# A two-block network on one core: the queue from which keys, queries and values are loaded back from DRAM

## The chip, the cores and the metric

The kernel runs on one core of a Trainium2 chip. The core has a matrix engine (TensorE, PE in the rows), a vector engine (VectorE, DVE), a scalar engine (ScalarE, ACT), a general engine (GpSimd, POOL) and SyncE (SP), which computes nothing and here only starts transfers. Each engine works off its own list of instructions in order; an instruction may wait for a semaphore that another engine or a transfer raises. A transfer between DRAM and the core's memory (SBUF) is started by an instruction on some engine's list and then runs beside it. The metric is the device time of the core, in microseconds (us); lower is better.

## The reference

The input is 512 tokens of width 1024, and for the second block 256 context tokens. Everything is fp32. In short:

```python
def first_block(x, c, ...):
    for l in range(2):                       # two hybrid layers
        h = rms_norm(x, gain) * (1 + scale) + shift        # scale, shift, gate from silu(c) @ w_mod
        aq, ak, av, ag, rq, rk, rv, rg, gq, gk, gv, gg, ga = split(h @ w_in)
        a = sliding_window_attention(rotary(aq), rotary(ak), av, sinks) * silu(ag)  # 8 heads, 2 of keys
        r = rms_norm(retention(rotary(rq), rotary(rk), rv)) * silu(rg)              # 4 heads
        g = rms_norm(gated_linear_attention(gq, gk, gv, log_a)) * silu(gg)          # GLA, 4 heads
        x = x + gate * rms_norm(concat([a, r, g]) @ w_out)

def second_block(x, c, ctx, ...):
    # layer 0, "even": windowed attention over tokens and context, and latent attention (8 heads),
    #   for the 512 tokens and for the 256 context tokens; then an FFN for each
    # layer 1, "odd": grouped attention (8 heads) and differential attention (4 heads)
    #   over context and tokens; then an FFN
    for l in range(2):
        h, hc = modulated rms_norm of x, xc
        y, yc = (mixer_even, mixer_odd)[l](h, hc, ...)
        x = x + g1 * rms_norm(y)
        x = x + g2 * rms_norm(swiglu(modulated rms_norm(x)))
        # layer 0 only: the same two steps for the context xc with yc
```

## The kernel before

The program is written in Python against a framework whose scheduler decides the order of each engine's list, from the order in which the code issues the operations and from its own estimate of when each will be ready. Pools of tiles with a fixed number of buffers set when a tile may be written again.

*Products.* Each fp32 operand is split into a high part that TensorE takes at its faster precision and a low part, the rest; a product is three matmuls (line 389: high x high, low x high, high x low). Weights come in units of 128 x up to 1024 elements. `weights` (lines 413 to 426) handles one: a transfer from DRAM into `wr` (line 417, three buffers), the high part `wh` by a cast on ACT (line 422, two buffers), the low part `wl` by a subtraction on POOL (line 398) or DVE (line 400). Some 370 such units pass in the whole program, so ACT has a cast of weights every few microseconds.

*Attention.* The projections give their results with features on the partitions, four heads to a tile. The rotation (`rope`) makes rotated pieces, each split in high and low. `put` (line 803) stores the pieces to a scratch tensor in DRAM, in an order that sorts them by head: `rq0`, `rk0`, `rv0`, `aq0`, `ak0`, `av0` for layer 0 of the first block, `rq1` and so on for layer 1, `eqm`, `eka`, `ekn`, `ekp`, `evb`, `eqc`, `eqpc` and others for the even layer, `oqc`, `okc`, `okd` and others for the odd one. `get` (line 806) loads the keys, queries and values of one head back into SBUF, where the products of attention and retention read them. Between a store and its get lies the wait for the store's landing in DRAM. The names on the left of a row are the tiles that a get fills: `rq`, `rk`, `rv` in retention (`retention`, line 1155), `wk`, `wq`, `wv` in the sliding windows, `ek`, `eq`, `ev` in the even layer's windows and latent attention, `ck`, `cq`, `cv` in the same for the context, `gk`, `gq`, `dk` in the odd layer.

*Stages.* In the first block, a layer projects (`layer1`), then runs GLA, whose chain of small steps is woven together with projections of the remaining units, with retention and with the sliding window. In a GLA step, ACT computes the exponentials of the decay factors (line 1068, tile `f`) and casts small operands (line 1087, tile `qb`). In the second block, projection, windows, latent attention, output projection and FFN follow each other; the context attention lies at about 900 to 980 us.

*Transfers.* Every transfer in the program stands on SP's list: the weight units, 128 transfers of modulation weights (line 738, tile `mr`) that come in the background, the stores, the gets, tables for the rotation (lines 1016 and 1024), and retention's decay masks (line 1165, into a buffer of tag `rq`). There are 1169 of them. The program counts their completions in eight counters, `DMAHW0` to `DMAHW7` in the rows of order, which it takes in turn: a transfer whose counter is still held by an earlier one waits for that one first.

```python
def put(self, dst, src):                                     # 802
    self.nc.sync.dma_start(dst, ...)                         # 803
def weights(self, src, n, where=None):                       # 413
    raw = self.tl(self.sb, [128, 1024], F32, "wr", 3)        # 415
    nc.sync.dma_start(raw[:, :n], src)                       # 417
    nc.scalar.copy(hi[:, :n], raw[:, :n])                    # 422
```

Of the kernel before, what the change touches and what calls it, by code (L numbers as in the profile page):

```python
# [11 lines left out]
F32 = mybir.dt.float32  # L12
# [187 lines left out]
class Net:  # L200
# [602 lines left out]
        self.nc.sync.dma_start(dst, src if src.dtype == F32 else src.bitcast(F32))  # L803

    def get(self, dst, src):
        self.nc.sync.dma_start(dst.bitcast(F32), src)

    def q_put(self, scr, pieces, h0, n=4, r=32):

# [1146 lines left out]
```

## Time and profile before

| what | value |
|---|---|
| device time, median of 3 runs | 2879.4 us (2874.68 to 2889.54) |
| the profiled execution: device time | 2882.13 us |
| its span, first to last instruction | 2880.3 us |
| mean granted clock of TensorE | 0.91 of full speed |
| busy, share of the span: PE, DVE, ACT, POOL | 86%, 44%, 41%, 37% |
| moved from and to DRAM | 398 MB, mean 139 GB/s |

Busy means that an instruction of that engine was being executed; starting a transfer, waiting and branching do not count. An engine's share is a mean over the whole span and hides stretches in which it is much busier. Of a transfer, the trace gives the time that its queue took to issue it and when its packets moved. The idle time ahead of an instruction is put down to what ended last before it: an instruction of another engine, a transfer, or "issue", when nothing that the profile shows was waited for.

### The profile page before, as it was taken

The page shows a single profiled execution, that of the slowest core. Times are in us where ns is not written, and L with a number is a line of the kernel's source. Part 1 is how long each engine was busy: PE and PEld are TensorE (multiplying, and loading weights), DVE is VectorE, ACT ScalarE, POOL GpSimd, SP SyncE. Part 2 cuts the span into 40 slices and gives each one's busy share as a digit, 9 for nine tenths or more (in the row PEclk, how much of TensorE's full clock was granted, in tenths as well). Part 3 has the DMA queues.
Part 4 walks back from the last instruction along what each step waited for, and adds up shares of the span by engine and source line. Part 5 has one row for each costly group of instructions (what it writes and reads, how often), then busy time and mean ns, then how long its engine had stood idle before and what let it go on. Part 6 is the DMA issues. An engine that isn't in the chain of part 4 may idle for free. (4 is left out here: it accounts for less than half of the span.)

```text
span 2880.3 us, 35460 instructions
## 1 busy us (share of the span) xinstructions
PE 2473.7 (86%) x13052; PEld 2008.7 (70%) x13052; DVE 1267.5 (44%) x2065; ACT 1187.0 (41%) x2227; POOL 1077.7 (37%) x754
## 2 busy tenths in 40 slices
PE   6887888677979987669999899999878969799997
PEld 4765566566657765548998777777766757588886
DVE  3645356335646644356453631222635647421212
ACT  2533355333537534346554422222434536333222
POOL 2434325334623551123455632323541221433334
PEclk9988889788989987779999999999888979899999
DMA  7454544435344553335653544453442254333332
GB/s 239 131 189 143 182 132 160 139 111 169 108 128 138 188 188 119 117 107 139 178 161 136 172 145 162 146 183 115 160 135 96 86 159 114 113 110 97 101 95 74
DMA packets 170817, 400.58 MB, mean 139 GB/s; under 512 B 19378, under 2 KB 60820, under 8 KB 167316
## 3 DMA queue, kind: packets, MB, share of 16 engines
q1 hardware_dynamic: 170644, 398.31, 42.6%
q8 instruction: 104, 1.70, 0.2%
q14 instruction: 69, 0.57, 0.1%
HBM read 339.85 MB, written 58.39 MB: 138 GB/s over the span
## 5 line engine op out<-in xcount | busy, mean ns | idle before, releaser
L398 POOL TENSOR_TENSOR wl<-wr,wh 128x1024 fp32r<-128x1024 f32 (+3 forms) x245 | 537.0, 2193 | 890.8 <-ACT wh L422 435.5
L422 ACT CAST wh<-wr 128x1024 fp32r<-128x1024 f32 (+3 forms) x367 | 353.4, 963 | 745.8 <-PE d L389 290.1
L389 PE MATMUL d<-hh,wh 128*128 128x512 f32 x960 | 405.6, 422 | 20.3 <-ACT hh L556 7.8
L389 PE MATMUL d<-hl,wh 128*128 128x512 f32 x960 | 399.1, 416 | 3.3 <-POOL hl L398 1.4
L389 PE MATMUL d<-hh,wl 128*128 128x512 f32 x960 | 261.8, 402 | 0.0
L400 DVE SCALAR_TENSOR_TENSOR wl<-wr,wh 128x1024 fp32r<-128x1024 f32 (+3 forms) x122 | 151.5, 1242 | 226.5 <-PE d L389 96.3
L389 PEld LDWEIGHTS d<-hh,wh 128*128 128x128 f32 x960 | 192.4, 200 | 72.1 <-issue 12.1
L389 PEld LDWEIGHTS d<-hl,wh 128*128 128x128 f32 x960 | 192.0, 200 | 45.9 <-issue 4.9
L389 PEld LDWEIGHTS d<-hh,wl 128*128 128x128 f32 x960 | 184.7, 194 | 40.6 <-issue 2.5
L921 POOL TENSOR_TENSOR oy<-pg,pg 64x256 f32<-64x256 f32 (+1 forms) x72 | 57.4, 797 | 299.9 <-DVE pg L919 95.6
L400 DVE SCALAR_TENSOR_TENSOR pg<-b,pg 128x512 fp32r<-128x512 f32 (+1 forms) x208 | 137.3, 666 | 67.7 <-ACT pg L404 66.1
L389 PE MATMUL b<-hh,wh 128*128 128x512 f32 x416 | 165.2, 397 | 0.0
L389 PE MATMUL b<-hl,wh 128*128 128x512 f32 x416 | 164.0, 394 | 0.0
L404 ACT CAST pg<-b 128x512 fp32r<-128x512 f32 (+1 forms) x208 | 117.3, 571 | 88.9 <-PE b L896 83.4
L869 DVE TENSOR_REDUCE sm<-s 128x1 f32<-128x768 f32 (+3 forms) x144 | 121.1, 847 | 65.0 <-PE s L389 64.2
L389 PE MATMUL d<-hc,wh 128*128 128x256 f32 x656 | 104.4, 309 | 24.9 <-DVE rp L400 12.5
L937 DVE SCALAR_TENSOR_TENSOR rp<-rp,d 128x512 f32<-128x512 f32 (+1 forms) x77 | 46.8, 607 | 165.0 <-ACT rp L936 164.9
L389 PE MATMUL d<-hid,wh 128*128 128x512 f32 (+1 forms) x528 | 117.6, 365 | 1.9 <-POOL hid L398 1.5
L1725 DVE SCALAR_TENSOR_TENSOR rp<-rp,b 128x512 f32<-128x512 f32 (+1 forms) x64 | 38.1, 595 | 175.8 <-PE b L389 175.3
L389 PEld LDWEIGHTS d<-hc,wh 128*128 128x128 f32 x656 | 94.0, 209 | 30.2 <-ACT wh L422 12.1
L389 PE MATMUL b<-hid,wh 128*128 128x512 f32 (+1 forms) x528 | 110.4, 360 | 0.0
L389 PEld LDWEIGHTS d<-hid,wh 128*128 128x128 f32 x528 | 90.1, 191 | 21.2 <-issue 2.9
(412 smaller groups left out, 5191.3 us busy)
## 6 DMA issues: line engine op xcount, KB each, us to landing
wr<-in_ffn_w_in SPq DMA_DIRECT2D x132, 512.0 KB
mr<-in_ada_w SPq DMA_DIRECT2D x96, 512.0 KB
wr<-in_ffn_w_out SPq DMA_DIRECT2D x48, 512.0 KB
x<-x SPq DMA_DIRECT2D x20, 1024.0 KB
wr<-in_w_in SPq DMA_DIRECT2D x38, 512.0 KB
mr<-in_w_mod SPq DMA_DIRECT2D x32, 512.0 KB
wr<-in_ev_w_in SPq DMA_DIRECT2D x20, 512.0 KB
wr<-in_ffn_w_out SPq DMA_DIRECT2D x24, 384.0 KB
```

The source lines that it names most:

```text
L389: self.nc.tensor.matmul(out, lhsT, rhs, start=start, stop=stop)
L398: self.nc.gpsimd.tensor_sub(out, src, hi)
L400: self.nc.vector.scalar_tensor_tensor(out, src, scale, hi, op0=ALU.mult, op1=ALU.subtract)
L404: self.nc.scalar.copy(hi, src)
L422: nc.scalar.copy(hi[:, :n], raw[:, :n])
L869: nc.vector.reduce_max(c, s, axis=AX.X, negate=True)
L921: nc.gpsimd.tensor_tensor(d, sel(t), sel(rs), op=ALU.mult)
L937: nc.vector.scalar_tensor_tensor(t, t, 1.0, ps, op0=ALU.add, op1=ALU.mult)
L1725: nc.vector.scalar_tensor_tensor(g, g, 0.5, pu, op0=ALU.mult, op1=ALU.mult)
```

## The change

```diff
--- before.py
+++ after.py
@@ -803,7 +803,7 @@
         self.nc.sync.dma_start(dst, src if src.dtype == F32 else src.bitcast(F32))
 
     def get(self, dst, src):
-        self.nc.sync.dma_start(dst.bitcast(F32), src)
+        self.nc.scalar.dma_start(dst.bitcast(F32), src)
 
     def q_put(self, scr, pieces, h0, n=4, r=32):
```

All 322 gets now stand on ACT's list; SP keeps 847 transfers, the stores among them. No instruction is added or removed. The scheduler orders every engine's list anew: 1125 rows of ACT's order differ, and 2306 of PE's. The pieces below give, for each instruction, its line, its operation, the tile it writes and the one it reads with the numbers that the program gives them, its size, and in brackets the semaphores that it waits for: `DMAHW` a transfer, `PE`, `DVE`, `Pool`, `Activation` an engine.

*Place 1: layer 1 of the first block, in GLA.* Before, SP's list reads as follows from the stores of retention's rotated queries to those of the keys:

```order
L803 DMA rq1_4256<-rp_1095_4928 4x32x512 [waits DVE_49]
L803 DMA rq1_4256<-rp_1101_4963 4x32x512 [waits DVE_49]
L417 DMA wr_1140_5169<-in_w_tok_b 128x768 [waits DMAHW5_49,DMAHW4_49]
L417 DMA wr_1143_5199<-in_w_tok_b 128x768 [waits DMAHW6_49,Pool_49]
L806 DMA rq_1180_5382<-rq1_4256 128x512 [waits DMAHW2_49,DMAHW3_49,DMAHW1_49,DMAHW0_49]
L1165 DMA rq_1183_5390<-in_decay 128x512 [waits DMAHW7_49]
L417 DMA wr_1166_5309<-in_w_in 128x1024 [waits Pool_49]
L803 DMA rk1_4257<-rp_1118_5052 4x32x512 [waits Activation_49]
L803 DMA rk1_4257<-rp_1110_5011 4x32x512 [waits DVE_49]
```

The first get here, row five, waits for the four counters of the stores above it; behind it stand the decay mask, a weight unit and the stores of the keys. The same get, of `rq_1180`, stands on ACT's list after the change, here between two casts of weight units:

```order
L404 CAST rp_1103_4969<-rp_1095_4928 128x512 [waits Pool_49]
L404 CAST rp_1104_4972<-rp_1101_4963 128x512 [waits DMAHW4_49,Pool_49]
L422 CAST wh_1135_5111<-wr_1134_5109 128x768 [waits DMAHW6_49,PE_49]
L806 DMA rq_1180_5382<-rq1_4256 128x512 [waits DMAHW2_49,DMAHW3_49,DMAHW1_49,DMAHW0_49]
L422 CAST wh_1138_5141<-wr_1137_5139 128x768 [waits DMAHW7_49,DVE_49,PE_49]
L1068 ACT_TABLE_LOAD
L1068 ACTIVATE f_1120_5062<-b_1121_5063 128x384 [waits PE_49]
```

It has moved behind the cast of `wh_1135` and ahead of that of `wh_1138` and of the exponentials of `f_1120`. A little further down ACT's list after the change, the four gets of the keys stand around two weight casts:

```order
L404 CAST pg_1175_5358<-pg_1173_5354 128x256 [waits Pool_49]
L806 DMA rk_1181_5384<-rk1_4257 64x512 [waits DMAHW7_49,DMAHW3_49,DMAHW1_49]
L422 CAST wh_1141_5171<-wr_1140_5169 128x768 [waits DMAHW4_49,PE_49,Activation_49]
L806 DMA rk_1181_5384<-rk1_4257 64x512 [waits DMAHW0_49]
L806 DMA rk_1182_5387<-rk1_4257 64x512 [waits DMAHW4_49,DMAHW2_49]
L806 DMA rk_1182_5387<-rk1_4257 64x512
L422 CAST wh_1144_5201<-wr_1143_5199 128x768 [waits DMAHW5_49,PE_49,Activation_49]
```

Three of the four gets lie between the casts of `wh_1141` and `wh_1144`; on SP they stood together, behind the tables of line 1016.

*Place 2: layer 0 of the first block, in GLA.* The difference of ACT's order, with the numbers of buffers left out, first at the queries of head 0 of retention:

```order
 L422 CAST wh_1082<-wr_1080 128x768
 L404 CAST pg_1238<-pg_1234 128x256
-L1087 CAST qb_130_775<-pg_1054 32x2x128 x4
+L1087 CAST qb_130_775<-pg_1054 32x2x128
+L806 DMA rq_1354<-rq_544 128x512
+L1087 CAST qb_130_775<-pg_1054 32x2x128 x3
 L404 CAST pg_1332<-pg_1328 128x256
```

The get has come between the first and the second of four small casts of GLA. Twenty rows further, at the keys of the same head:

```order
 L404 CAST rp_1028<-rp_1019 128x512
 L422 CAST wh_1142<-wr_1140 128x768
-L1087 CAST qb_128_773<-pg_1236 32x2x128 x4
+L806 DMA rk_1356<-rk_545 64x512 x2
+L806 DMA rk_1359<-rk_545 64x512 x2
+L1087 CAST qb_128_773<-pg_1236 32x2x128 x3
 L422 CAST wh_1172<-wr_1170 128x768
+L1087 CAST qb_128_773<-pg_1236 32x2x128
```

The four key gets have come ahead of the next four casts of this kind. For the next head, ACT's order after the change, from the cast that feeds a store of the attention's keys (`ak0`) to the decay factors:

```order
L404 CAST rp_232_1312<-rp_233_1313 128x512 [waits DMAHW5_49,Pool_49]
L806 DMA rk_323_1671<-rk0_545 64x512 [waits DMAHW6_49,PE_49]
L806 DMA rq_322_1669<-rq0_544 128x512 [waits DMAHW0_49,PE_49]
L404 CAST pg_283_1491<-pg_282_1489 128x128 [waits DVE_49,Activation_49]
L806 DMA rk_323_1671<-rk0_545 64x512 [waits DMAHW2_49]
L806 DMA rk_324_1674<-rk0_545 64x512 [waits DMAHW4_49]
L806 DMA rk_324_1674<-rk0_545 64x512 [waits DMAHW6_49]
L806 DMA rv_326_1679<-rv0_548 128x4x128 [waits DMAHW7_49,PE_49]
L1068 ACTIVATE f_286_1499<-b_287_1500 128x384
L1068 ACTIVATE f_286_1499<-b_288_1504 128x384
```

Queries, keys and values of the head are now loaded from here, and the last get, of `rv_326`, waits for counter `DMAHW7` ahead of the exponentials of `f_286`. On SP's list after the change the stores that these wait for stand here:

```order
L738 DMA mr_285_1498<-in_w_mod 128x1024 [waits DMAHW3_49,DMAHW0_49,PE_49]
L738 DMA mr_300_1558<-in_w_mod 128x1024 [waits DMAHW5_49,DMAHW4_49,PE_49]
L803 DMA ak0_547<-rp_232_1312 2x32x512 [waits Activation_49]
L803 DMA ak0_547<-rp_232_1312 2x32x512 [waits DMAHW7_49]
L803 DMA ak0_547<-rp_233_1313 2x32x512 [waits DMAHW1_49,DVE_49]
```

The second store of `ak0` is the one that takes counter `DMAHW7`; it stands behind two transfers of modulation weights.

*Place 3: the context attention of the second block.* A piece of the difference of ACT's order, at the context's queries, keys and values:

```order
+L806 DMA ck_7460<-eka 64x256 x2
+L806 DMA ck_7463<-eka 64x256 x2
 L623 COPY y_6703<-d_7383 128x512
+L806 DMA cq_7466<-eqc 128x256
+L806 DMA cq_7468<-eqc 128x256
+L806 DMA cq_7470<-eqc 128x256
+L806 DMA cq_7472<-eqc 128x256
+L806 DMA cv_7474<-eva 128x2x128
+L806 DMA ck_7563<-eka 64x256
 L503 ACTIVATE rp_7458<-oy_6699 128x512
+L806 DMA ck_7563<-eka 64x256
+L806 DMA ck_7566<-eka 64x256 x2
```

Gets come in ahead of the exponential of line 503 and of the softmax that follows it, eleven in this piece; 86 lie in this stretch in all.

## Rows read from the trace of the kernel before

**Rows 1.** Page, part 1: busy time, share of the span and count of each engine.
```profile
PE 2473.7 (86%) x13052; PEld 2008.7 (70%) x13052; DVE 1267.5 (44%) x2065; ACT 1187.0 (41%) x2227; POOL 1077.7 (37%) x754
```

**Rows 2.** Two windows: length, busy time and count per engine, then clock, DMA share, GB/s.
```profile
560.00:810.00 250.00, 198.86 (x935) 156.61 (x934) 123.23 (x208) 100.91 (x205) 108.08 (x96) 0.88 0.40 131
900.00:980.00 80.00, 70.72 (x393) 55.99 (x393) 45.61 (x99) 50.61 (x141) 33.25 (x32) 0.94 0.57 180
```

**Rows 3.** Line 806: ns to issue (minimum/median/maximum), first and last start; who waited for it.
```profile
L806 SPq DMA_DIRECT2D ck<-ekn x32: 444/567/597, 915.9 to 965.7; - x32
...
L806 SPq DMA_DIRECT2D cq<-eqpc x16: 444/590/1681, 918.9 to 957.8; - x16
...
L806 SPq DMA_DIRECT2D cv<-evb x8: 376/380/587, 920.1 to 970.7; - x8
...
L806 SPq DMA_DIRECT2D eq<-eqm x8: 319/432/4920, 1079.3 to 1167.2; - x8
...
  PE s L389: 47.0, 7
```

**Rows 4.** Waits of SP's queue: us in total, times, longest, by what was awaited.
```profile
SPq L806 <- PE s L389: 41.0, 22, 10.0
...
SPq L806 <- DMA rq<-rp: 19.2, 5, 6.2
SPq L806 <- DMA oqc<-rp: 18.7, 3, 10.7
```

**Rows 5.** Timeline of SP's queue, layer 1's GLA: start us, us, instructions joined in xcount.
```profile
636.02 1.19 SPq L803 DMA_DIRECT2D rq<-rp  x1
637.31 3.31 SPq L417 DMA_DIRECT2D wr<-in_w_tok_b  x2
648.69 0.33 SPq L806 DMA_DIRECT2D rq<-rq  x1
...
650.01 3.56 SPq L803 DMA_DIRECT2D rk<-rp  x4
...
662.72 3.95 SPq L806 DMA_DIRECT2D rk<-rk  x4
```

**Rows 6.** Timeline of ACT, the same stretch; in brackets idle time before and releaser.
```profile
638.91 0.84 ACT L422 CAST wh<-wr 128x768 fp32r<-128x768 f32 x1 [3.39 <-PE d L389]
...
652.02 0.83 ACT L422 CAST wh<-wr 128x768 fp32r<-128x768 f32 x1
654.05 0.83 ACT L422 CAST wh<-wr 128x768 fp32r<-128x768 f32 x1 [1.19 <-issue]
```

**Rows 7.** Timeline of SP's queue, layer 0's GLA and retention.
```profile
138.47 0.33 SPq L806 DMA_DIRECT2D rq<-rq  x1
...
154.17 3.64 SPq L806 DMA_DIRECT2D rk<-rk  x4
...
203.30 1.12 SPq L803 DMA_DIRECT2D ak<-rp  x2
```

**Rows 8.** Timeline of ACT, layer 0's GLA and retention.
```profile
131.27 1.68 ACT L1087 CAST qb<-pg 32x256 fp32r<-32x256 f32 x4
...
149.57 1.69 ACT L1087 CAST qb<-pg 32x256 fp32r<-32x256 f32 x4
...
199.63 0.87 ACT L1068 ACTIVATE f<-b 128x384 f32<-128x384 f32 x2
```

**Rows 9.** Timelines of SP and of ACT, even window attention.
```profile
1097.04 0.32 SPq L806 DMA_DIRECT2D eq<-eqm  x1
...
1090.81 0.27 ACT L404 CAST rp<-b 128x128 fp32r<-128x128 f32 x1
```

**Rows 10.** Odd grouped attention: waits of PE, timelines of SP and of ACT.
```profile
PE s L389 <- DMA gq<-oqc: 10.1, 1, 10.1
...
2158.03 1.75 SPq L806 DMA_DIRECT2D gq<-oqc  x4
...
2148.77 0.37 ACT L404 CAST rp<-s 128x256 fp32r<-128x256 f32 x1 [1.16 <-PE s L389]
```

## The prediction

> **What bounds the kernel now.** I read the busy shares first. TensorE (PE) is busy 86% of the span, ScalarE (ACT) 41% [rows 1]: PE sets the time and ACT looks half idle. But the share is an average, and the gets all lie in the attention and GLA stretches, so I read two of these by window. In the stretch of layer 1's GLA and retention, PE is busy 198.9 of 250 us; in the context attention ACT is busy 50.6 of 80 us, far above its mean [rows 2]. So the question is not whether ACT has room in 2880 us, but whether it has room, and nothing urgent behind it, where the gets are put.
>
> **What a get costs on SyncE (SP).** The view of the line that issues the gets groups the 322 transfers by what they load. Each takes about half a microsecond to issue: the two largest groups of the context attention, 32 and 16, have medians of 0.567 and 0.590. One took 4.92 us to issue, when the queue was full [rows 3]. Before a get can be issued, its data must have landed in DRAM: the waits of SP's queue show 19.2 us for the store of the retention's queries, 18.7 us for the odd layer's queries, and 41.0 us for PE to finish with the buffer that a get overwrites [rows 4]. All of this now stands on SP, which computes nothing. PE in turn waited 47.0 us for gets, 7 times [rows 3].
>
> **What the change moves.** The pieces of the order above show it: the 322 gets leave SP's list and stand between ACT's casts and exponentials, where the scheduler believes that their data will be ready. Nothing is added or removed. ACT's list is worked off in order, so a get whose store has not landed holds every cast behind it. How late the stores are is read from before's own rows.
>
> *Layer 1's GLA.* The last store of the rotated queries was issued at 636.02, and the get followed at 648.69 with nothing issued from 640.62 on: SP stood and waited for the landing, some 12 us after the store [rows 5]. In the new order this get stands ahead of ACT's cast of a weight unit, which ran at 638.91 [rows 6]. So that cast moves to 648.69 + 0.33 = 649.0: ACT halts 10.1 us. Queued behind are that weight unit, which PE's projection waits for, the exponentials of the decay factors, and the casts that feed the next stores. Those stores therefore shift too, so the next halt adds: the gets of the keys were issued from 662.72 to 666.67 [rows 5], and stand before and behind the weight cast of 652.02, the last three ahead of that of 654.05 [rows 6]. 666.67 - 654.05 = 12.6 us. Together **22.7 us**.
>
> The Trainium skill says in "DMA: Bandwidth & Descriptors", section "Anatomy of one DMA", that DMA engines do not wait on semaphores: the wait is on the issuing sequencer, before dispatch. The trace agrees, with SP's 8.1 us without an issue; by this rule the halt would come at each such get, and it is the rule that speaks most against this change.
>
> *Layer 0's GLA.* The first get stands behind the first of four casts that begin at 131.27 (each 0.42) [rows 8]; its data landed when SP issued it at 138.47 [rows 7]: 138.47 + 0.33 - 131.69 = 7.1 us. The four key gets, 154.17 to 157.81, stand ahead of the cast of 149.57: 8.2 us. The third place is a new wait. The program gives its transfers eight completion counters in turn, and a transfer waits for the last one on its counter, whichever queue that is on. The get of the next head's values waits for counter 7, which a store of the attention's keys holds; that store is issued from 203.30 on [rows 7], and takes no less than the 662.72 - 653.57 = 9.2 us from the last key store's issue to its landing in [rows 5]. Behind the get stand the factors' exponentials, at 199.63 before [rows 8]: 203.30 + 9.2 + 0.5 - 199.63 = 13.4 us. Together **28.7 us**.
>
> *Context attention.* 86 of the gets fall into 80 us. 32 at 0.567, 16 at 0.590, and 38 others at 0.38 to 0.59 [rows 3] are 42 to 50 us; I take 46. With ACT's 50.6 busy [rows 2] that is 97 of 80 us: ACT becomes the bound of this stretch, **17 us** over. No row shows whether ACT's unit works on while its sequencer issues a transfer. If it does, this term is 0; if the issue is dearer on ACT than on SP, it is larger. I take SP's price, the nearest row.
>
> *Even window.* The first get of the second head group stands ahead of a cast that ran at 1090.81; its data had landed at 1097.04 [rows 9]: **6.6 us**.
>
> *Odd grouped attention.* The get of the queries was issued at 2158.03, and in the new order stands ahead of a cast of 2148.77: 9.6 us. But PE itself waited 10.1 us for just this transfer [rows 10], so I count **0**.
>
> These are 22.7 + 28.7 + 17 + 6.6 = 75 us of halt on ACT. The other gets stand at places of the same kind, or in ACT's idle time; for them I take 20 us, between 0 and the 41.0 us that SP waited for PE's buffers. Of 95 us, PE loses what it would have been doing: 198.9 of 250 us busy is 80%, so 76 us. **What comes back:** SP has 322 issues less and its weight loads need not queue behind a waiting get. The bound is the 47.0 us that PE waited for gets, but these waits end with the landing of a store, as at 648.69 and 2158.03, and this does not come earlier; and where a get held a weight load on SP, it now holds the cast that would split that weight. I take 10 us. Net +66 us. The profiled execution took 2882.1 us (span 2880.3), so 2948; it lies 2.7 us above the median of the three runs, so **2945 us**.
>
> **Rivals.** (1) *Faster.* SP's queue is the tight place: PE gets its 47 us back, 2882 - 47 = 2835, median 2832. For it: SP stood over 8 us at 640 while weight loads were queued behind. Against: those loads' casts now stand behind the same wait on ACT. It decides where ACT's halts lie inside ACT's own idle time, as in the odd grouped attention. Chance 0.09. (2) *No difference*, 2865 to 2894: ACT idles 59%, and halts of 5 to 13 us are caught up. For it: the halts lie in stretches where ACT waits a lot too, 3.39 us ahead of the cast of 638.91. Against: the casts behind the gets feed PE's next product, not a store. The Trainium skill, same page, section "Issuing engines are not separate DMA queues", has a rule that would end here: issuing from several engines only saves the sequencer's time, usually little against the transfer. That an issue is short agrees with [rows 3], but the rule leaves out what the wait ahead of the issue does to a computing engine. Chance 0.09. (3) *Much slower*, over 3040: nothing of the issue is hidden, so 322 at 0.57 = 184 us less the 46 counted adds 138 us to the 75 and the 41, 2882 + 254 = 3136; a full queue holds ACT 4.92 us as it held SP once. Against: over the whole span ACT has 1690 us idle. Chance 0.08. That the change does not do what it says is excluded by the order: every get is on ACT's list.
>
> **Numbers.** The forecast, ACT halted and PE with it by 5 to 160 us, has 0.74. Something like 0.5% (14 us) is what a measurement of this kernel can tell from no change. Slower holds the forecast and rival 3: 0.82; same 0.09; faster 0.09. The range reaches from 2885, where almost everything is absorbed, to 3040, where the forecast's 75 and 41 us come through whole and a third of the 138 us of issues with them (75 + 41 + 45 = 161, 2879 + 161 = 3040); it leaves out the faster case, most of the unchanged one and rival 3.
>
> **What would show it.** Right: a second queue of DMA with 322 issues on ACT; ACT idle for 10 us or more ahead of the weight cast or the factors' exponentials in both GLA stretches, ended by a store's landing; PE's waits for ACT there grown; the context attention stretched to about 95 us; the stretches without gets (the FFNs) as long as before. Wrong: gets on ACT that wait under 2 us, or PE's gaps in these stretches no longer than before. The prediction fails if the stores land earlier once SP issues them with no get ahead, or if ACT works on during an issue.

## The result

The changed kernel takes 2960.96 us (median of 4 runs, 2955.32 to 2964.66) against 2877.9 us (4 runs, 2874.68 to 2889.54): a ratio of 1.0279, 95% interval 1.0246 to 1.0313, some 80 us more. The forecast was 2945 us, slower with a chance of 0.82, range 2885 to 3040. The profiled execution took 2955.32 us; its span is 2953.5 us, 73.2 us more than before.

The page of the profile after, its busy times and its DMA queues:

```profile
PE 2481.5 (84%) x13052; PEld 2019.1 (68%) x13052; DVE 1264.8 (43%) x2065; ACT 1189.1 (40%) x2227; POOL 1077.1 (36%) x754
...
q10 hardware_dynamic: 51488, 57.43, 6.8%
```

DVE, ACT and POOL are busy for as long as they were, within 3 us [rows 1]; PE is busy for 7.8 us more. There is a second queue, q10, which is ACT's, and the rest of the 73 us is idle time of PE. Where it lies, a table by stage shows. I cut the span of before into nine stretches and put each cut, in the trace of after, where the same PE instruction (the n-th with this line and these tiles) stands. Length, then busy time and count of PE, PEld, DVE, ACT and POOL, then clock, DMA share and GB/s; before:

```profile
0.00:560.00 560.00, 442.16 (x2287) 332.67 (x2288) 274.56 (x488) 231.65 (x485) 208.51 (x180) 0.87 0.49 164
560.00:900.00 340.00, 274.22 (x1330) 218.31 (x1328) 170.33 (x299) 150.60 (x339) 139.13 (x124) 0.89 0.40 127
900.00:1000.00 100.00, 89.14 (x515) 71.27 (x516) 58.39 (x121) 60.83 (x165) 45.67 (x43) 0.93 0.57 192
1000.00:1250.00 250.00, 191.21 (x1004) 153.75 (x1003) 122.48 (x233) 105.57 (x216) 79.32 (x59) 0.82 0.38 132
1250.00:1500.00 250.00, 216.99 (x1543) 195.98 (x1543) 124.36 (x182) 133.86 (x238) 92.18 (x55) 0.92 0.53 154
1500.00:2060.00 560.00, 544.51 (x3006) 446.81 (x3004) 178.06 (x250) 191.65 (x278) 228.51 (x125) 0.98 0.45 151
2060.00:2340.00 280.00, 227.65 (x1179) 191.73 (x1179) 148.69 (x212) 122.53 (x219) 94.55 (x62) 0.88 0.36 119
2340.00:2480.00 140.00, 118.64 (x579) 94.65 (x580) 92.54 (x154) 77.85 (x147) 40.18 (x29) 0.89 0.50 147
2480.00:2880.00 400.00, 369.20 (x1619) 303.57 (x1617) 98.14 (x128) 112.44 (x142) 149.65 (x81) 0.96 0.29 92
```

After:

```profile
0.00:558.00 558.00, 438.82 (x2287) 334.76 (x2288) 272.81 (x488) 231.90 (x485) 208.32 (x180) 0.87 0.50 164
558.00:912.60 354.60, 275.36 (x1329) 221.92 (x1328) 169.76 (x299) 150.09 (x339) 138.07 (x124) 0.87 0.38 122
912.60:1032.50 119.90, 96.25 (x515) 74.74 (x516) 57.56 (x121) 61.99 (x165) 46.42 (x43) 0.89 0.48 159
1032.50:1286.40 253.90, 188.19 (x1004) 150.89 (x1002) 123.27 (x233) 105.34 (x216) 79.28 (x59) 0.82 0.38 130
1286.40:1558.00 271.60, 218.23 (x1542) 197.85 (x1543) 126.23 (x182) 134.28 (x238) 92.38 (x55) 0.89 0.47 142
1558.00:2115.50 557.50, 541.48 (x3006) 443.68 (x3005) 178.27 (x250) 191.69 (x278) 228.65 (x125) 0.99 0.45 151
2115.50:2397.80 282.30, 228.70 (x1187) 193.31 (x1187) 146.71 (x210) 121.12 (x216) 92.54 (x60) 0.88 0.35 118
2397.80:2552.50 154.70, 124.54 (x571) 98.04 (x572) 92.06 (x156) 80.10 (x150) 41.91 (x30) 0.84 0.43 133
2552.50:2953.00 400.50, 369.93 (x1619) 303.90 (x1617) 98.11 (x128) 112.57 (x142) 149.54 (x81) 0.95 0.29 92
```

Read the second number, the length, row by row. Layer 0 of the first block: -2.0. Layer 1: +14.6. Output projection with the context attention: +19.9. Even projection and window: +3.9. Latent attention: +21.6. FFN: -2.5. Odd projection and grouped attention: +2.3. Differential attention: +14.7. The rest: +0.5. The sum is 73.0. The stretches without gets cost nothing, as the forecast had it. And in the context attention PE's busy time rose too, from 89.1 to 96.3 for the same 515 matmuls, at a granted clock of 0.89 instead of 0.93.

The line of the gets after (the columns as in [rows 3]):

```profile
L806 ACTq DMA_DIRECT2D ck<-ekn x32: 452/470/617, 940.9 to 1006.6; - x32
L806 ACTq DMA_DIRECT2D ek<-ekn x32: 452/458/2156, 1317.6 to 1512.5; - x32
...
  PE s L389: 42.5, 17
```

An issue takes about as long on ACT as on SP: these 32 transfers are shorter (0.470 against 0.567 us), others are longer (`ck<-eka` 0.605 against 0.468). In this row, the products into `s`, PE still waits 42.5 us for gets, 17 times instead of 7 [rows 3]. The 47 us that the faster rival wanted back did not come.

### The profile page after: what moved, and what is told of

Read it like the earlier page. It is cut to its first block, busy times and chain, and to the rows that moved or that the text cites. A ratio compares the mean times of both kernels' runs of the same rounds, so it can differ in the third digit from the quotient of the medians.

```text
span 2953.5 us, 35388 instructions
## 1 busy us (share of the span) xinstructions
PE 2481.5 (84%) x13052; PEld 2019.1 (68%) x13052; DVE 1264.8 (43%) x2065; ACT 1189.1 (40%) x2227; POOL 1077.1 (36%) x754
## 5 line engine op out<-in xcount | busy, mean ns | idle before, releaser
L389 PE MATMUL d<-hh,wh 128*128 128x512 f32 x960 | 398.6, 415 | 22.0 <-DVE rp L937 10.8
L389 PE MATMUL d<-hl,wh 128*128 128x512 f32 x960 | 391.7, 408 | 0.9 <-DVE hl L557 0.9
L389 PE MATMUL d<-hc,wh 128*128 128x256 f32 x656 | 104.7, 308 | 26.3 <-ACT wh L422 12.8
L483 POOL TENSOR_TENSOR sm<-sm,mhalf 128x4 f32<-128x4 f32 (+3 forms) x33 | 45.4, 1377 | 178.1 <-DVE sm L481 177.8
```

Of the source, the lines that this page charges most:

```text
L389: self.nc.tensor.matmul(out, lhsT, rhs, start=start, stop=stop)
L483: nc.gpsimd.tensor_tensor(r, ms, self.mhalf[:, None, :].to_broadcast([128, nt, n]), op=ALU.pow)
```

## The experiments

### Where the cost sits: the gets of some stages at a time

The three kernels give the gets of some stages to ACT and leave the others on SP; the names stand for the buffers of a stage.

```diff
         def area(self, pool, name, **bufs):
-
+        self.via = self.nc.scalar if name + "p" * ("kp" in bufs) in ("cp",) else self.nc.sync
...
-        self.nc.sync.dma_start(dst.bitcast(F32), src)
+        self.via.dma_start(dst.bitcast(F32), src)
```

With `("cp",)`, the context attention:

> Only the 86 gets of the context attention (even_ctx_window and even_latent over the context) are started by ScalarE, the other 236 stay on SyncE. In the changed kernel matched PE instructions fell behind by 17 to 20 us between 900 and 980 us of before. Theory A (each place costs what it costs by itself: halts on ScalarE and the time of issuing there): 15 to 22 us slower than before, and nowhere else a shift of over 3 us. Theory B (the new order of the whole program costs, wherever it moved anything): under 8 us. Theory C (the rival of no difference, idle time takes the halts up): within 5 us.

With `("r", "w")`, the first block:

> Only the 84 gets of the first block (retention and sliding window, both layers) are started by ScalarE. Theory A: layer 1 costs 12 to 16 us, as in the changed kernel, and layer 0 nothing or a gain of up to 7 us, since its halts of 7.3, 8.0 and 9.0 us fall where PE does not wait for ScalarE: 5 to 16 us slower in all. The prediction's working (four fifths of every halt reach PE) would give 28.7 + 22.7 = 51.4 us of halts and 41 us slower. Theory B: under 5 us.

With `("e", "ep", "g", "d")`, the rest of the second block:

> Only the 152 gets of the even layer's window and latent attention over tokens and of the odd layer are started by ScalarE. Theory A: the rest of the 83 us, by the shifts of matched PE instructions in the changed kernel: even window 4 to 6, latent attention 17 to 22, odd layer 15 to 20: 33 to 45 us slower. The prediction's working (6.6 us for the even window, 0 for the grouped attention, a lump of 20 us for all other gets, four fifths of it): 21 us. Theory B: the three parts together come to far less than 83 us, so under 25 here.

Measured against 2881.99 us: 2906.11 us (1.0083, 1.0055 to 1.0112), 2895.58 us (1.0054, 1.0036 to 1.0072) and 2921.99 us (1.0140, 1.0110 to 1.0169). The three excesses add up to 2.77%, and all gets together cost 2.79%. So theory A holds in the main: each place costs what it costs by itself, and theory B, a price of the new order as a whole, falls. The context attention's part came out above theory A's range, 24.1 us against 15 to 22. In its trace PE falls back by 20.4 us in this stretch itself, and by 3 us more in the even window, where theory A wanted no such shift. The first block costs 13.6 us where the prediction's working gives 41; the rest of the second block 40.0 us where it gives 21.

In the context attention alone, a part of the loss is PE's clock. The same stretch of work, about 175 matmuls, before and in this kernel (columns as in the table by stage):

```profile
952.00:983.00 31.00, 28.20 (x177) 21.76 (x176) 15.40 (x41) 18.24 (x51) 14.35 (x13) 0.96 0.60 195
```

```profile
955.00:1003.00 48.00, 35.75 (x174) 26.38 (x173) 16.63 (x44) 20.95 (x57) 13.05 (x12) 0.79 0.54 164
```

PE had 2.8 us of idle time in 31.0 us and ran at 0.96; with the gets on ACT it has 12.3 us of idle time in 48.0 and runs at 0.79, a mean between its two levels (2.4 and 1.2 GHz), and the same matmuls take 35.75 us instead of 28.20. Of the 17 us, 9.5 are idle time and 7.5 are busy time; the ratio of the clocks alone would make 34.3 of the 28.20 (28.20 x 0.96 / 0.79), so some 6 of the 7.5 go with the clock.

### Is it the wait for the landing?

The prediction's largest terms were gets on ACT that wait for a store to land. Two kernels take the landing away: one 128x1024 piece (`twin`, the high part of a weight unit) is stored once near the start, and every get reads that.

```diff
     def get(self, dst, src):
+        src = self.twin[:dst.shape[0], :math.prod(dst.shape[1:])]
+        src = src.rearrange("p (t d) -> p t d", d=128) if len(dst.shape) == 3 else src
-        self.nc.sync.dma_start(dst.bitcast(F32), src)
+        self.nc.scalar.dma_start(dst.bitcast(F32), src)
```

> All gets are started by ScalarE, but read a 128x1024 scratch that is written once near the start, not the stored queries, keys and values; so no get waits for a landing, only for the buffer that it fills, and the output is not the reference's. To be compared with the same on SyncE (next run). Theory H (the price is the halt for a landing): the two take the same, within 10 us. Theory L (a get goes out late, since ScalarE's list holds work ahead of it that itself waits for TensorE, and TensorE then waits for the data) and theory I (the time of issuing on ScalarE): the second block's part stays, 45 to 70 us more than on SyncE, and only the 15 us of the first block go.

The second has the added lines, but `nc.sync` as before:

> The same reading of one early scratch, with the gets on SyncE as before. TensorE waited 47.0 us for gets before. If those were waits for the landing, this kernel is 15 to 45 us faster than before; if they were waits for buffers or for the queue, within 10 us of it.

Measured against 2878.41 us: 2916.22 us on ACT (1.0135, 1.0120 to 1.0151) and 2838.89 us on SP (0.9870, 0.9853 to 0.9886). On SP the landing is worth 39.5 us, as expected of PE's 47.0 us of waits. But the step from SP to ACT costs 77.3 us without that landing, about what it costs with one. Theory H falls as the explanation of the whole. Nor did the first block's part go, as theories L and I wanted: at 900 us PE is 18 us later on ACT than on SP. ACT's timeline of this kernel in layer 1 shows why the halts did not go:

```profile
600.00 3.14 ACTq L812 DMA_DIRECT2D rk<-twin  x4
604.68 0.33 ACTq L812 DMA_DIRECT2D rv<-twin  x1
605.12 1.04 ACT L423 CAST wh<-wr 128x1024 fp32r<-128x1024 f32 x1 [12.46 <-DMA rk<-twin]
```

ACT was idle for 12.46 us ahead of the weight cast, five gets being in front of it: 7.3 us until the first one went out at 600.00, the rest while the five were issued. The order of this kernel says what they wait for; first three stores on SP's list, then ACT's:

```
L807 DMA eqnc_3893<-rp_1038_4630 2x64x256 [waits DMAHW4_49,DVE_49]
L807 DMA eqpc_3894<-rp_1043_4648 8x16x256 [waits DMAHW5_49,Activation_49]
L807 DMA eqpc_3894<-rp_1046_4659 8x16x256 [waits DMAHW7_49,Activation_49]
...
L423 CAST wh_1058_4762<-wr_1057_4760 128x544 [waits DMAHW7_49,PE_49,Activation_49]
L1093 CAST qb01_1079_4849<-q_954_4265 32x2x128 x2
L812 DMA rk_1181_5386<-twin_190 64x512 [waits DMAHW4_49]
L812 DMA rk_1181_5386<-twin_190 64x512 [waits DMAHW5_49]
L812 DMA rk_1182_5389<-twin_190 64x512 [waits DMAHW7_49]
L812 DMA rk_1182_5389<-twin_190 64x512 [waits DMAHW0_49]
L812 DMA rv_1184_5394<-twin_190 128x512 [waits DMAHW2_49]
```

By this order each get waits for its completion counter and nothing else, and counters 4, 5 and 7 were last taken by the three stores. So a landing still holds ACT, that of a transfer which this get has nothing to do with.

### What does the issue cost by itself?

Here the gets stay on SP. ACT starts a copy into a scratch that nothing reads, beside each get: of the stored piece (first kernel), or of the early 128x1024 piece (second kernel, with the store of `twin` and the two lines above that set `src`).

```diff
     def get(self, dst, src):
         self.nc.sync.dma_start(dst.bitcast(F32), src)
+        ghost = self.scr(list(src.shape), self.name("ghost"))
+        self.nc.scalar.dma_start(ghost[tuple(slice(None) for _ in src.shape)], src)
```

> Every get stays on SyncE; beside each, ScalarE starts a copy of the same stored piece into a DRAM scratch that nothing reads. So ScalarE pays for 322 issues and for the waits for the stores' landing, but TensorE's data come by SyncE as before; the copies wait for no buffer and stand a little earlier on ScalarE's list than the gets of the changed kernel did. Theory L (the get goes out late from a busy list): within 25 us of before. Theory I (issue time) or H (halt for the landing): 40 to 85 us slower.

> The same 322 copies on ScalarE, but of one 128x1024 scratch that is written once near the start: issues of the same number and shapes with no landing to wait for, wherever the scheduler puts them; the gets stay on SyncE. Theory I: 322 issues at some 0.5 us cost 40 us or more. Theory L: -5 to +15 us. The difference to the run before is what the landing's halts cost by themselves.

Measured against 2878.61 us: 3007.75 us (1.0460, 1.0433 to 1.0487) and 2960.79 us (1.0284, 1.0259 to 1.0309). So 322 copies on ACT with no stored data to wait for cost 82 us, 0.26 us for each. The copies of the stored pieces cost 129 us, more than any of the three theories gave. The 47 us between the two are not the landing alone, since the copies stand at other places of the list. Theory L alone, that only the late data cost, falls. The line of these copies, and the largest sum of ACT's idle time that ended with one:

```profile
L814 ACTq DMA_DIRECT2D ghost<-twin x322: 475/477/1406, 25.4 to 815.3; - x161
...
ACT pg L405 <- DMA ghost<-twin: 25.5, 5, 6.6
```

The scheduler put all of them ahead of 815 us, often several in a row; in the row shown, such a run held a cast for up to 6.6 us. They do not stand where the gets of the changed kernel stood, they take their turn at the counters, and they add traffic; no run has the same copies on SP, which would tell the traffic's part. The 0.26 us is therefore a price in this program, and not the share of the issue in the 80 us.

### Gets further ahead on ACT's list

If the second block's gets merely go out too late on ACT, moving them up should help.

```diff
+        self.lead = 300 if name + "p" * ("kp" in bufs) in ("cp", "ep", "g", "d") else 0
...
-        self.nc.sync.dma_start(dst.bitcast(F32), src)
+        with self.ahead(self.lead): self.nc.scalar.dma_start(dst.bitcast(F32), src)
```

> The changed kernel, with the gets of the second block given to the scheduler 300 steps ahead, so that they stand earlier on ScalarE's list (a head's gets together and ahead of the last two or three exponentials of the head before, not spread behind them); as many issues as in the changed kernel. Theory L: the second block's 64 us shrink by a quarter or more, 2920 to 2945 us. Theory I: nothing changes, 2953 to 2967. Theory H, with the wait for a buffer in place of the landing: slower still, over 2967.

Measured: 3011.6 us (1.0472 of before, 1.0449 to 1.0494), 51 us slower than the changed kernel. Theory L's forecast had the wrong sign; theory H's "over 2967" came true, but the longest halt in the context attention was no wait for a buffer. ACT's timeline there:

```profile
905.18 1.75 ACTq L806 DMA_DIRECT2D ckp<-ekp  x4
...
918.92 0.39 ACTq L806 DMA_DIRECT2D cv<-eva  x1
919.35 0.58 ACT L912 COPY pg<-d 64x512 f32<-64x512 f32 x1 [13.66 <-DMA cq<-eqc]
```

Here 22 gets stand together and are issued one behind the other, and ACT is idle for 13.66 us ahead of the copy of line 912. PE's waits for the copies of line 918 in this stage rise from 2.2 to 15.9 us, while its waits for the gets' data stay as they were (5.1 against 5.3 us). So here moving the gets up bought nothing at the data and cost at ACT.

### Other engines, other transfers

Gets on GpSimd (`self.nc.gpsimd.dma_start` in `get`):

> The gets are started by GpSimd. If what costs is that a get stands in line behind a computing engine's work, this is slower too: GpSimd's mean weight subtraction takes 2.2 us against ScalarE's 1.0 us for a cast, but it has 754 instructions against 2227, so 30 to 110 us slower than before. If the price is special to ScalarE (its exponentials and casts are what TensorE waits for), within 25 us of before.

Measured: 2910.01 us against 2878.61 (1.0111, 1.0088 to 1.0135). Slower too, but by 31 us, some 40% of what ACT costs. In layer 0 PE ran up to 12.8 us ahead of before; at the end of the first block it was 4 us behind, and the rest of the loss is the second block's. The engine is not all that differs: the page lists the queue of these gets as `software_dynamic`, ACT's and SP's as `hardware_dynamic`. What that alone does, no run here shows.

Stores on ACT, gets on SP (`self.nc.scalar.dma_start` in `put`):

> The gets stay on SyncE; instead the stores (line 803, some 216 rows of the order) are started by ScalarE. A store waits for a subtraction or a cast, not for a landing in DRAM. If the cost of the change is the halt for the landing, the stores cost less than half of it: between 15 us faster and 25 us slower. If it is the time of issuing on a computing engine, 216 of 322 of the 83 us: some 55 us slower.

Measured: 2885.81 us against 2881.99 (1.0018, 1.0002 to 1.0033). Not 55 us: the price belongs to the place. PE ran 26 us ahead by the end of layer 0 and lost it in layer 1, the even projection and the odd layer. That pointed to a faster kernel, in which only the stores of the first block, and of the context's projection woven into it, are on ACT:

```diff
+        self.put_by = self.nc.scalar             # at the start
...
-        self.nc.sync.dma_start(dst, src if src.dtype == F32 else src.bitcast(F32))
+        self.put_by.dma_start(dst, src if src.dtype == F32 else src.bitcast(F32))
...
+        self.put_by = nc.sync                    # ahead of the second block
```

> The gets on SyncE as before; the stores of the first block and of the context's projection that is woven into it are started by ScalarE, the later ones by SyncE. With all stores on ScalarE, matched PE instructions ran ahead of before by 20 to 26 us from 400 to 1040 us and lost it again in the even layer's projection. If what ScalarE's list holds ahead of a transfer decides place by place, this is 15 to 27 us faster than before. If each transfer on ScalarE has a price of its own, it is 5 us slower or more.

Measured: 2861.19 us against 2878.41 (0.9938, 0.9925 to 0.9951), 17 us faster than before. In its trace one halt stands out, early in layer 0:

```profile
105.37 0.35 ACTq L804 DMA_DIRECT2D gate<-rp  x1
105.77 0.82 ACT L1088 CAST qb<-q 32x256 fp32r<-32x256 f32 x2 [10.07 <-DMA angles<-pg]
```

The gate store stands between the sixth and the seventh of eight casts of this kind. The order gives what it waits for, `L804 DMA gate0_550<-rp_94_567 128x512 [waits DMAHW6_49,DVE_49]`, and on SP, `L1009 DMA angles_514<-pg_80_487 4x32x512 [waits DMAHW6_49]`: the store of a rotation table holds counter 6. So the gate stores went back to SP (`nc.sync.dma_start` in place of `self.put` in line 1261):

> The stores of the first block on ScalarE as two calls ago, but the eight gate stores of each layer back on SyncE. There ScalarE stood 10.07 us at 95 us ahead of a gate store whose data had long been ready: its completion counter was held by a store of the rotation tables on SyncE. Matched PE instructions lost 8 to 13 us at 88 to 160 us. If the shared counter is the cause, that halt goes and the kernel is 5 to 14 us faster than that version, 22 to 32 us faster than before. If the halt is the scheduler's order or just moves to the next transfer on ScalarE, the gain stays at 12 to 20 us.

All eight casts of line 1087 (1088 here) then run through; the last four:

```profile
94.02 1.69 ACT L1088 CAST qb<-q 32x256 fp32r<-32x256 f32 x4 [0.20 <-DVE qb L1055]
```

So that halt came with the gate store on ACT; that the counter held it is read from the order and from the releaser in the row. The total is 2859.02 us against 2880.15 (0.9926, 0.9907 to 0.9946), 21 us faster than before, between the two forecasts, and not to be told from the 17 us of the version with the halt: PE is 10 us ahead of the version with the halt until 260 us and has given it back by 400. What else holds layer 0 there, no run shows.

## Why the prediction was right, and where it was not

**Layer 1: the halts were where it put them, the loss came from elsewhere.** ACT's timeline after:

```profile
649.07 0.32 ACTq L806 DMA_DIRECT2D rq<-rq  x1
649.51 0.83 ACT L422 CAST wh<-wr 128x768 fp32r<-128x768 f32 x1 [14.44 <-DMA rq<-rp]
...
666.39 0.48 ACTq L806 DMA_DIRECT2D rk<-rk  x1
666.99 0.83 ACT L422 CAST wh<-wr 128x768 fp32r<-128x768 f32 x1 [5.30 <-DMA rk<-rp]
...
669.96 0.83 ACT L422 CAST wh<-wr 128x768 fp32r<-128x768 f32 x1 [2.14 <-DMA rk<-rk]
```

Forecast were 10.1 us more of idle time ahead of the first weight cast and 12.6 us around the next two. Measured were 14.44, and 5.30 + 2.14; but before had 3.39 us ahead of the first cast and 1.19 ahead of the last already [rows 6], so the change added 11.05 and 6.25. The first halt was right. The step "Those stores therefore shift too, so the next halt adds" was too dear: the first get of the keys went out 3.7 us later than before (666.39 against 662.72), not 10.1, and the cast of 654.05 came 15.9 us later, not 22.7.

PE fell behind with these halts (instructions matched as in the table by stage, times of before): its product of 653.98 started 13.9 us later, at 667.87. But it won most of that back at once. Before, in ACT's timeline and in PE's, and then after, in PE's:

```profile
670.76 1.04 ACT L422 CAST wh<-wr 128x1024 fp32r<-128x1024 f32 x1 [7.20 <-DMA wr<-in_w_in]
...
674.52 1.01 PE L389 MATMUL b<-mod_sel,ms 128*128 128x2 f32 x4 [7.26 <-ACT ms L723]
```

```profile
681.97 0.61 PE L389 MATMUL b<-mod_sel,ms 128*128 128x2 f32 x4 [0.31 <-ACT ms L723]
```

Before, SP issued this weight load at 666.72, right behind the gets of the keys [rows 5]; ACT waited 7.20 us for it, and PE 7.26 us for a copy that stands behind this cast on ACT's list. After, PE waited 0.31 us there. So the same landing was paid for before too, on another list. The kernel with the early scratch on SP bears this out: without that landing PE gains 6 us at 665 to 675. By 720 us PE was 2.9 us behind. It lost 8 us more at 750, at a halt that the working had no term for, two gets of the next head's keys and one of its values:

```profile
753.63 0.40 ACT L404 CAST pg<-pg 128x256 fp32r<-128x256 f32 x1 [10.20 <-DMA rk<-rk]
```

The stage's 14.6 us therefore lie close to the forecast's 18 (0.8 times 22.7) by luck; of what the named halts did, little was left at its end.

**Layer 0: the halts held, their effect did not last.** The three places, get and following row each:

```profile
136.54 0.34 ACTq L806 DMA_DIRECT2D rq<-rq  x1
136.93 1.25 ACT L1087 CAST qb<-pg 32x256 fp32r<-32x256 f32 x3 [7.25 <-DMA rq<-rp]
...
155.08 4.26 ACTq L806 DMA_DIRECT2D rk<-rk  x4
159.38 1.25 ACT L1087 CAST qb<-pg 32x256 fp32r<-32x256 f32 x3 [8.02 <-DMA rk<-rk]
...
209.87 0.56 ACTq L806 DMA_DIRECT2D rv<-rv  x1
210.48 0.87 ACT L1068 ACTIVATE f<-b 128x384 f32<-128x384 f32 x2 [8.99 <-DMA ak<-rp]
```

Forecast 7.1, 8.2 and 13.4 us; measured 7.25, 8.02 and 8.99. The third is the counter that a store of the attention's keys holds, named in brackets. Yet the stage is 2.0 us shorter than before. The halts did reach PE: from 2.0 us ahead of before it fell 8 us behind after the second one, and 12 us after the third. But it was ahead again by 175 us, and level by 250. The weight cast behind the second halt shows how, before and after:

```profile
166.11 1.04 ACT L422 CAST wh<-wr 128x1024 fp32r<-128x1024 f32 x1 [11.74 <-DMA wr<-in_w_in]
```

```profile
164.40 1.04 ACT L422 CAST wh<-wr 128x1024 fp32r<-128x1024 f32 x1 [2.48 <-DMA wr<-in_w_in]
```

Before, SP issued this weight load at 159.56, behind the gets of the keys, which it had issued from 154.17 to 157.81 [rows 7], and ACT waited 11.74 us for it; after, the load was issued at 155.05, with no get ahead of it on SP's list. Without the landing, on SP, PE gains 9.2 us just there, at 160 to 175. Two steps failed. "Of 95 us, PE loses what it would have been doing": a busy share of 80% does not say what of a halt is left a hundred microseconds on. And "I take 10 us" for what comes back: the sentence before it has the mechanism, a get that held a weight load on SP now holds the cast of that weight, but takes it for a reason why little comes back. It means that the halt stands in place of one that before had already: some 10 us came back behind the keys' gets of layer 0 alone, and 11 in layer 1 by 720 us. The second rival's mechanism, halts caught up, is right for layer 0 whole and for the named halts of layer 1 in the main.

**Context attention: the size held, the working only in part.** Forecast 17 us of ACT, 13.6 of PE (0.8 of it); measured 19.9 for the stage and 20.4 in the trace with these gets alone. The forecast assumed that ACT is occupied by every issue, and names it as a sign of failure "if ACT works on during an issue". ACT's timeline shows both halves:

```profile
924.91 0.59 ACT L623 COPY y<-d 128x512 f32<-128x512 f32 x1 [1.69 <-DMA ck<-eka]
924.93 2.89 ACTq L806 DMA_DIRECT2D cq<-eqc  x4
927.86 0.45 ACTq L806 DMA_DIRECT2D cv<-eva  x1
928.35 0.49 ACTq L806 DMA_DIRECT2D ck<-eka  x1
928.88 0.63 ACT L503 ACTIVATE rp<-oy 128x512 f32<-128x512 f32 x1 [3.39 <-DMA cq<-eqc]
```

The copy of 924.91 runs while the issues of 924.93 begin: ACT's unit works on what it was given already, but gets nothing new. Four, one and one issues in a row then leave it idle for 3.39 us. Sums of idle time that a get ended, in the table of ACT's waits for this stretch, come to 19.3 us (4.2, 3.4, 3.0, 2.7, 2.3, 2.0 and 1.7), not to 46. Of PE's 19.9 us, 12.8 are idle time and 7.1 busy time (table by stage), at the lower clock.

**The lump was mis-sized.** "The other gets ... for them I take 20 us" stood for 16 us of PE's time. Measured: latent attention 21.6, differential attention 14.7, together 36.3; and the halt of 10.20 us in layer 1 was one of these gets too. The differential attention's part is spread over many waits of PE of 0.8 to 1.6 us, and no row names one cause. In the latent attention the cost is not a halt of ACT but a get that goes out late. PE's waits for the queries there, before and after:

```profile
PE s L389 <- DMA eq<-eqnm: 3.1, 1, 3.1
```

```profile
PE s L389 <- DMA eq<-eqnm: 23.3, 4, 8.3
```

Before, the first `ek` went out at 1273.1 us; after, at 1317.6, and PE's work had shifted by 36.4 us until then: 8.1 us late, behind what ACT had to do first. Whether the lateness, the length of six to eight issues in a row, or the wait for a buffer weighs most in the second block's 64 us (24 + 40), these runs do not settle; moving the gets up made it worse, so it is not the lateness alone.

**Small terms.** Even window: 6.6 forecast, 3.9 for its stage. Odd grouped attention: 0 forecast for a halt of 9.6; ACT's halt was 8.0 and the stage lost 2.3. The stores did not land earlier with no get ahead of them, the other sign of failure: the keys' get of layer 1 followed the last issue of its stores by 8.5 us, against 9.2 before.

So the sign and the range held, and the first halt of each layer stood where the rows had it, with the size that they gave. That 2945 lies near 2961 is luck: layer 0 was too dear by 25 us (0.8 times 28.7 against -2.0) and layer 1 by 4, the context attention was too cheap by 6 and the later gets by 20.

The Trainium skill, "DMA: Bandwidth & Descriptors", section "Issuing engines are not separate DMA queues", says that issuing from several engines saves only the time on the sequencer, which is usually small. The traces agree on the size, 0.470 us an issue of the row above. What the runs add is the other side: on an engine that computes, that time is a price, and 322 copies with no stored data to wait for made the kernel 82 us slower, their turns at the counters and their traffic included.

## What to carry to other kernels

A transfer on a computing engine's list is an instruction like any other: what counts is what stands behind it, whether that is on the path, and which counters it shares with slow stores elsewhere. Judge it place by place: the same engine was a loss for loads that others wait for (80 us) and a gain for the first block's stores (17 us). A busy share is no measure of how much of a halt is left. Ask what waited for the same landing before: where another list paid for it already, as SP's did for the weight loads in GLA, the halt is not new, and most of it comes back.

## What the hardware showed that I had not expected

- ACT was idle for 12.46 us around five gets whose data had long landed, and for 10.07 us ahead of a gate store whose data were ready; by the order, what they waited for were completion counters held by unrelated stores on the other queue.
- ACT's unit works on during an issue, on the instruction that it has: at 924.91 a copy of 0.59 us covered the first of six issues in a row, and the other five left ACT idle for 3.39 us.
- Idle gaps came with a second loss on TensorE: in the context attention's last part, with these gets alone on ACT, 9.5 us more of idle time came with a clock of 0.79 instead of 0.96 and 7.5 us more of busy time.
